# A fused RWKV-7 and HGRN2 layer on one core: bank order in the planner, the last column blocks of the output projection, and the layer norm

## The chip, the core and the metric

The kernel runs on one core of one Trainium2 chip. A core has five engines with instruction queues of their own: TensorE (PE, with weight loads shown as PEld) for matrix products, VectorE (DVE) and ScalarE (ACT) for elementwise work, GpSimd (POOL), and SyncE (SP), which here only issues DMA transfers. Each engine works through its queue in program order. Operands lie in SBUF; matrix products are summed up in PSUM, which has eight banks of 512 float32 columns on 128 partitions. The metric is device time in microseconds for one call, as the median of several runs. A profiled execution is a run of its own; its rows have times from the start of its span.

## What is computed

One layer with two groups of heads that read the same input `x` of 512 tokens by 2048 features: RWKV-7 time mixing and HGRN2 gated linear recurrence. Their gated outputs stand side by side and pass through one output projection, a residual and a layer norm:

```python
proj = einsum('btd,dc->btc', h, w_in)             # 2048 -> 8320 columns
o_rwkv = rwkv7(token_shift(proj[..., :RWKV_COLS])) * silu(z_r)
o_hgrn = hgrn2(proj[..., RWKV_COLS:]) * silu(z_h)
y = einsum('btc,cd->btd', concatenate([o_rwkv, o_hgrn], -1), w_out)
h = layer_norm(ALPHA * h + y, ln_w, ln_b)
```

The layer norm takes mean and variance of a token's 2048 values, then `(v - mean) * rstd * ln_w + ln_b`.

## The kernel before

**Products.** All large products are made with float32 values split in two float32r halves, hi and lo. `split` (L361) writes hi on ScalarE (`act` with a copy, in the trace L301) and lo = raw - hi on VectorE (`tt`, L311). `three` (L391, matmuls at L396) adds hi x hi, hi x lo and lo x hi into one PSUM bank, so each product costs three matmuls of 128 x 128 weights against 512 or 256 columns.

**Weights.** `load(j)` (L376) brings one row of `w_all`, 512 KB, into one of two raw buffers (`wr`). Each holds two quarters of 512 columns. `ready(i)` asks for the split of quarter i into a `wh` and a `wl` buffer (three of each); when the second quarter of a load is split, the load after the next goes out from SP's queue into the same buffer. `part(i)` waits, in the planner's time, until quarter i is split.

**The planner.** A class `Plan` writes the program order of all engines while the kernel is built. It keeps a clock per engine and for each tile when it was last written (`ready`) and last used (`busy`). Small tasks are Python generators in queues (`splits`, `evacs`, `scans`, `heads`, `sums`, `norms` and others); after each main matmul `pump` takes from them what could start by now. `start` gives the earliest start of an operation, `best` picks among the engines that could do it (a copy can go to ScalarE or VectorE), `issue` writes it down. For a read, `start` looks only at when the tile was written. For a write it also looks at the last use, but a write by TensorE looks at it only where the bank was just taken anew. The waits that the program has on the chip are placed by the framework from the real order of accesses; the planner's times only choose order and engine.

**Order of the work.** Projections run one after another on TensorE, and between their matmuls stand the small products of the RWKV scans (`rwkv_scan`, L288 and L292 in the trace), and of the HGRN2 heads. In a scan step the bank `pd` holds two results side by side: VectorE folds one into the state (`bd`), and copies of the other go to `z`. The bank `px` is read by a subtraction (`rt`), a copy and two additions (`t`).

**Output projection.** Its 2048 columns are done in five blocks, of 512, 512, 512, 256 and 256 columns. In the first four, `rows` runs over 16 steps of the inner dimension (eight of two for the 256 block), and in each over the four groups of 128 tokens, so four banks are open and the four token groups end close together. While the fourth block runs, the weights of the fifth are split too, some into free `t` buffers (`early`, `IN_T`). The fifth goes token group by token group, outermost, with all its weights there.

**Evacuation and norm.** `row_out` adds the residual (`xr`, loaded by `residual` from SP's queue) to a finished bank on VectorE (`stt`, L320), then takes statistics (`bn_stats`, L1336) and multiplies by `ln_w` (`premultiply`, L333, VectorE or GpSimd). After the fifth block of a token group, `finish` aggregates the statistics (L1279), and takes rstd as a power on GpSimd (L343). Then the columns are finished in two ways. `early`: the first `POOL_COLS[t]` columns are scaled and shifted on ScalarE (L1294), multiplied and added on GpSimd (L336), and written by SP. `late`: the others get two `scalar_tensor_tensor` on VectorE (less mean times weight, then times rstd plus bias) and are written from ScalarE's queue (L1310).

Of the kernel before, what the change touches and what calls it, by code (L numbers as in the profile page):

```python
# [15 lines left out]
P = 128  # L16
# [36 lines left out]

SETS = {AF.Sigmoid: ("sigmoid",), AF.Tanh: ("exp", "sigmoid"), AF.Exp: ("exp",)}


class Plan:
# [11 lines left out]
    def __init__(self, room):  # L69
        self.clock = {"pe": 0.0, "dve": 0.0, "act": 0.0, "pool": 0.0, "dma": 0.0}  # L70
        self.table = None
        self.narrow = False
        self.queues = []
        self.ready, self.busy = {}, {}
        self.room = room
        self.slots = {tag: [(0, 0.0)] * n for tag, n in room.items()}
        self.count, self.used = 0, {}

    def start(self, e, op):

        t = 0.0
        for r in op.reads:
            t = max(t, self.seen(r, e))
        for w in op.writes:
            x, by = self.busy.get(w, (0.0, e))
            if e != "pe" or by is None:
                t = max(t, x if by == e else x + self.AFTER[by])
        return t

# [117 lines left out]
def mixer_kernel(ctx, tc, x_t, x_r, w_all, par, up, ln_wb, consts, hmask, out):  # L207
# [25 lines left out]
    def take(tag, shape=(P, T), dt=F32):  # L233

        if not plan.free(tag):
            raise RuntimeError(f"no room: {tag}")
        slot = min(plan.slots[tag])
        plan.slots[tag].remove(slot)
        if tag in PBUFS:
            t = ppool.tile(list(shape), dt, tag=tag, name=nm(tag), bufs=PBUFS[tag])  # L240
        else:
            t = st(tag, list(shape), dt)
        name = t.tensor.name
        plan.busy[name] = (slot[1], None)
        tags[name] = tag
        return t
# [132 lines left out]
    def ready(i, tags=("wh", "wl")):  # L379
# [58 lines left out]
    def rows(q, width, lh, ll, fin, order=range(KT), hook=None, tags=("main",), early=None):  # L438
# [3 lines left out]
        for j in range(KT // per):  # L442
# [3 lines left out]
            for t in range(4):  # L446
                if j == 0:
                    pss.append(main_ps(tags)[:, :width])
                if early:
                    for i in early[j][t - 1 : t]:  # L450
                        ready(q + i, ("t", "t") if i in IN_T else ("wh", "wl"))
                elif 0 < t < 3:
                    ready(q + j + t)
# [614 lines left out]
    def first(q, tag):  # L1068
# [10 lines left out]
        def bring(c0, c1):  # L1079
# [3 lines left out]
            def run():  # L1083
                if q not in parts:
                    parts[q] = tuple(st(t, [P, QT], F32R) for t in ((tag, tag) if tag else ("wh", "wl")))
                hi, lo = parts[q]
# [161 lines left out]
    sums, earlies, norms = plan.queue(), plan.queue(), plan.queue()  # L1248
    stats = cpool.tile([P, 4, 5, 6], F32, tag="stats", name="stats")
# [3 lines left out]
    POOL_COLS = (768, 640, 512, 512)  # L1253
    blocks = [(0, 512), (512, 512), (1024, 512), (1536, 256), (1792, 256)]
# [6 lines left out]
    def cuts(c0, c1):  # L1261

        return [(max(c0, d * T), min(c1, d * T + T)) for d in range(4) if max(c0, d * T) < min(c1, d * T + T)]

# [3 lines left out]
    def premultiply(t, c0, c1):  # L1268

        c0 = max(c0, POOL_COLS[t])  # L1270
        if c0 < c1:
            y, w = ys[t][c0 // T][:, c0 % T : (c1 - 1) % T + 1], lnw[0][:, 0, c0:c1]
            k = y_keys(t, c0, c1)
            yield keyed(Op([dve_tt_way(y, y, w), pool_tt_way(y, y, w)], [], []), k, k)

    def finish(t):
        mv, rs = take("mv", [P, 4]), take("rs", [P, 1])
        k_st, k_mv, k_v, k_n, k_r, k_m = ([f"{n}{t}"] for n in ("stat", "mean", "var", "neg", "rstd", "bias"))
        yield keyed(Op([("dve", 0.1, lambda: dve.bn_aggr(mv[:, 0:2], stats[:, t]))], [], []), k_st, k_mv + k_v)  # L1279
        yield keyed(ts(mv[:, 1:2], mv[:, 1:2], LN_EPS, None, ALU.add), k_v, k_v)  # L1280
        yield keyed(ts(mv[:, 2:3], mv[:, 0:1], -1.0, None, ALU.mult), k_mv, k_n)
        yield keyed(rsqrt(rs, mv[:, 1:2]), k_v, k_r)

        def columns(c0, c1):
            y = ys[t][c0 // T][:, c0 % T : (c1 - 1) % T + 1]
            return y, lnw[0][:, 0, c0:c1], lnw[0][:, 1, c0:c1], out[t * P : t * P + P, c0:c1], y_keys(t, c0, c1)

        def early():

            yield keyed(pool_tt(mv[:, 3:4], mv[:, 2:3], rs, ALU.mult), k_n + k_r, k_m)  # L1290
            for c0, c1 in cuts(0, POOL_COLS[t]):
                y, w, b, o, k = columns(c0, c1)
                n = c1 - c0
                yield keyed(Op([("act", 0.28 + n * 0.00083, lambda: sc_e.activation(  # L1294
                    y, y, AF.Identity, scale=rs, bias=mv[:, 3:4]))], [], []), k + k_r + k_m, k)
# [19 lines left out]
    last_cols = (blocks[4][0], D)  # L1315

    def row_out(t, b, ps, xr, last=True):
        c0, n = blocks[b]
        d, o = c0 // T, c0 % T
        if o == 0:  # L1320
            ys[t][d] = yt[4 * t + d]
        y = ys[t][d][:, o : o + n]
        k = y_keys(t, c0, c0 + n)

        def run():
            yield keyed(stt(y, xr[:, o : o + n], ALPHA, ps, ALU.mult, ALU.add),
                        [xr.tensor.name, ps.tensor.name], k + [y.tensor.name])
            drop(ps)
            if last:
                drop(xr)  # L1330
            plan.add(sums, rest())
            if b == 4:
                plan.add(sums, finish(t))

        def rest():
            yield keyed(Op([("dve", 0.07 + n * 0.00105, lambda: dve.bn_stats(stats[:, t, b], y))], [], []),  # L1336
                        k, [f"stat{t}"])
            if b < 4:
                yield from premultiply(t, c0, c0 + n)
# [3 lines left out]
    def residual(t, c0, n):  # L1343
        xr = take("g")
        nc.sync.dma_start(xr, x_r[t, :, c0 : c0 + n])
        plan.fetched(xr, 4 * n)
        return xr

    xrs = {}

    def fin(t, ps, b):
        c0, n = blocks[b]
        if b == 0 and t == 0:
# [3 lines left out]
        row_out(t, b, ps, xrs[t], n == T)  # L1357

    def ahead(j, b):

        if b == 0:
# [6 lines left out]
        c0, n = blocks[b]  # L1368
        t = j - (KT // 2 if n == T else 0) - 3
        if 0 <= t < 4:  # L1370
            plan.until(room(g=1))
            xrs[t] = residual(t, c0, T)


    IN_T = (3, 4, 8, 9, 10, 11, 12, 13)
    early = ((2, 3, 4), (5,), (6,), (7, 8), (9, 10), (11, 12), (13, 14), (15,))
    for b in range(4):
        w = blocks[b][1]
        rows(4 * unit(w // P), w, gh, gl, lambda t, ps, b=b: fin(t, ps, b), korder, lambda j, b=b: ahead(j, b),
             ("main", "acc", "mix") if b else ("main",), early if b == 3 else None)  # L1380


    last = 4 * unit(2)
# [10 lines left out]
def _layout(inputs):  # L1394
# [72 lines left out]
```

## Time and profile before

| | us |
|---|---|
| median of three runs (lowest to highest) | 1121.27 (1120.59 to 1122.06) |
| the profiled execution | 1123.09 |
| its span, first to last instruction | 1121.3 |
| granted clock of TensorE, mean | 0.991 |

The profiled execution is 1.8 us over its span and 1.8 us over the median. In the rows of the profile, a group has its line, engine, operation, `out<-in` by the program's names, shape, count, then busy time, mean of one in ns, and the idle time before it with what ended it. A timeline row has start, duration and the same names. The name `q` or `inv` in the last stage is an output tile, `g` the residual, `big` the layer norm's weight and bias.

### The profile page before, as it was taken

To read this page: it belongs to the slowest core of one execution; us is meant where nothing else is said; L and a number is where in the kernel's file an instruction comes from. 1 tells how busy PE (TensorE), PEld (TensorE's weight loads), DVE (VectorE), ACT (ScalarE), POOL (GpSimd) and SP (SyncE) were. 2 spreads that over 40 slices of the span, in tenths; PEclk is the share of its full clock that TensorE was granted. 3 is DMA by queue.
4 is the path that set the end of the run, shared out by engine and by line. 5 is a ranking of instruction groups with operands and counts; after the bars stand their busy time and mean duration, and the time that the engine had idled before them with its cause. 6 is when DMAs were issued, how large, how long until landed. Compare 5 with 4: busy or idle time off the path is not lost.

```text
span 1121.3 us, 19205 instructions
## 1 busy us (share of the span) xinstructions
PE 1091.5 (97%) x7402; PEld 901.8 (80%) x7402; DVE 766.5 (68%) x1739; ACT 456.3 (41%) x1042; POOL 88.6 (8%) x163
## 2 busy tenths in 40 slices
PE   8999999999999999999999999999999999999994
PEld 7878878788888878788887888888887778888893
DVE  6658967645579767857986774657976776624468
ACT  6532365433332465534245552433346444322221
POOL 0000000000010000101000010001000010000015
PEclk8999999999999999999999999999999999999997
DMA  7222211133323311223231122322231145433433
GB/s 274 85 80 93 95 59 58 57 99 94 90 75 103 96 58 59 67 79 117 76 104 58 58 76 87 99 92 77 94 102 46 52 141 194 136 122 110 144 126 138
DMA packets 36667, 108.50 MB, mean 97 GB/s; under 512 B 4320, under 2 KB 6496, under 8 KB 36448
## 3 DMA queue, kind: packets, MB, share of 16 engines
q1 hardware_dynamic: 34848, 104.33, 29.2%
q10 hardware_dynamic: 1728, 2.95, 0.7%
q8 instruction: 58, 0.95, 0.4%
q14 instruction: 33, 0.27, 0.1%
HBM read 99.92 MB, written 7.34 MB: 96 GB/s over the span
## 4 chain that ended last, share of the span: by engine, by line
PE 89%; DVE 6%; ACT 2%; issue 1%; DMA 1%; POOL 0%; SPq 0%; DVEq 0%; ACTq 0%
PE main L396 68%; PE mix L288 10%; PE mix L396 3%; PE acc L396 3%; PE acc L288 3%; PE mix L292 2%; DVE q L320 1%; DVE wl L311 1%; DVE t L311 1%; ACT z L301 1%; DVE bd L320 1%; ACT wh L301 1%; DMA t<-x_t 0%; DVE inv L320 0%; DMA t<-spill 0%
## 5 line engine op out<-in xcount | busy, mean ns | idle before, releaser
L396 PE MATMUL main<-xh,wh 128*128 128x512 f32 x896 | 358.0, 400 | 2.2 <-ACT xh L301 2.2
L396 PE MATMUL main<-xh,wl 128*128 128x512 f32 x896 | 356.6, 398 | 0.0
L396 PE MATMUL main<-xl,wh 128*128 128x512 f32 x896 | 356.0, 397 | 0.0
L301 ACT ACTIVATE wh<-wr 128x512 fp32r<-128x512 f32 (+1 forms) x313 | 195.5, 626 | 268.9 <-PE main L396 203.9
L311 DVE TENSOR_TENSOR wl<-wr,wh 128x512 fp32r<-128x512 f32 (+1 forms) x313 | 213.5, 683 | 130.2 <-ACT wh L301 126.9
L396 PEld LDWEIGHTS main<-xh,wh 128*128 128x128 f32 x896 | 169.1, 189 | 36.0 <-ACT xh L301 2.6
L396 PEld LDWEIGHTS main<-xl,wh 128*128 128x128 f32 x896 | 168.9, 188 | 33.8 <-DVE xl L311 0.8
L396 PEld LDWEIGHTS main<-xh,wl 128*128 128x128 f32 x896 | 168.9, 189 | 33.5
L396 PE MATMUL main<-wh,xh 128*128 128x512 f32 (+1 forms) x272 | 108.0, 397 | 1.9 <-DVE t L320 1.9
L396 PE MATMUL main<-wh,xl 128*128 128x512 f32 (+1 forms) x272 | 108.1, 397 | 0.0
L396 PE MATMUL main<-wl,xh 128*128 128x512 f32 (+1 forms) x272 | 107.4, 395 | 0.0
L301 ACT ACTIVATE z<-mix 64x64 f32<-64x64 f32 (+1 forms) x245 | 56.0, 229 | 92.1 <-DVE bd L320 71.4
L396 PEld LDWEIGHTS main<-wh,xh 128*128 128x128 f32 x272 | 51.3, 189 | 10.4 <-DVE t L320 2.3
L396 PEld LDWEIGHTS main<-wh,xl 128*128 128x128 f32 x272 | 51.3, 189 | 8.6
L396 PEld LDWEIGHTS main<-wl,xh 128*128 128x128 f32 x272 | 51.3, 189 | 8.2
L302 ACT ACTIVATE t<-main,om 128x512 f32<-128x512 f32 x33 | 22.6, 688 | 61.2 <-PE main L396 61.1
L320 DVE SCALAR_TENSOR_TENSOR bd<-mix,pc,bd 64x64 f32<-64x64 f32 x112 | 31.2, 283 | 22.4 <-PE mix L288 17.2
L343 POOL TENSOR_TENSOR rs<-rs,mhalf 128x8 f32<-128x8 f32 (+1 forms) x16 | 25.1, 1572 | 250.3 <-DVE rs L316 129.5
L311 DVE TENSOR_TENSOR inv<-inv 64x30 f32<-64x30 f32 (+14 forms) x120 | 38.6, 322 | 3.1
L311 DVE TENSOR_TENSOR inv<-inv,inv 64x30 f32<-64x30 f32 (+14 forms) x120 | 38.6, 322 | 2.9
L346 POOL MEMSET z<- 64x128 f32 x64 | 11.9, 199 | 355.7 <-PE acc L288 312.1
L311 DVE TENSOR_TENSOR t<-t,tot 128x256 f32<-128x256 f32 x96 | 38.4, 416 | 0.2
(207 smaller groups left out, 1489.1 us busy)
## 6 DMA issues: line engine op xcount, KB each, us to landing
wr<-w_all SPq DMA_DIRECT2D x158, 512.0 KB, 3.5
t<-x_t SPq DMA_DIRECT2D x16, 256.0 KB, 5.6
g<-x_r SPq DMA_DIRECT2D x16, 256.0 KB, 4.2
spill<-g SPq DMA_DIRECT2D x12, 256.0 KB, 4.3
t<-spill SPq DMA_DIRECT2D x12, 256.0 KB, 4.0
big<-ln_wb SPq DMA_DIRECT2D x1, 2048.0 KB, 9.1
out<-q ACTq DMA_DIRECT2D x7, 256.0 KB, 2.4
up<-up SPq DMA_DIRECT2D x8, 128.0 KB, 2.8
```

The source lines that it names most:

```text
L288: return Op([("pe", cost, lambda: pe.matmul(o, l, r, start=start, stop=stop, **kw))], [l, r], [o], narrow=narrow)
L292: return Op([("pe", 0.11, lambda: pe.transpose(o, i, ident))], [i], [o])
L301: return "act", cost, lambda: sc_e.activation(o, i, f, scale=scale)
L302: return "act", cost, lambda: sc_e.activation(o, i, f, scale=scale, bias=bias)
L311: return dve_op([a, b], o, lambda: dve.tensor_tensor(o, a, b, f), base=0.16 if o.shape[0] < P and size(o) == C and o.tensor.name in tags e ...
L320: return dve_op([a, b], o, lambda: dve.scalar_tensor_tensor(o, a, s, b, f1, f2), per=0.00113, base=0.085 if o.shape[0] == P else 0.25 if s ...
L343: lambda: pool.tensor_tensor(o, i, mhalf[:, : size(o)], ALU.pow))], [i], [o])
L346: return Op([("pool", 0.1, lambda: pool.memset(o, v))], [], [o])
L396: pe.matmul(ps, l, r, start=first and i == 0, stop=last and i == 2)
```

## The change

Three things are changed.

1. **Planner.** PSUM banks are noted in `plan.banks`. A read of a bank may start only when the last use of that bank by another operation has ended (`done`), not only when it was written, and a write by TensorE takes account of the last use by another engine.
2. **Last two column blocks.** The output projection has four blocks of 512 columns. The first two run as before through `rows`. The third runs with token groups innermost, and in between the weights of the fourth are split, by quarters in the order of `_last_quarters`: (2, n) is a quarter of the third block, (3, n) one of the fourth. Those of the fourth go into `t`, `ksq` and `ia` buffers (`home`) and, for the last three, into `wh` and `wl`. The fourth runs with token groups outermost: 48 matmuls of 512 columns each. Its residual is loaded at the fourth of sixteen steps.
3. **Layer norm.** The multiplications and additions on GpSimd are gone. For token groups 0 to 2, ScalarE scales and shifts each of four 512-column pieces, and VectorE multiplies by the weight and adds the bias. For the last group the first two pieces (`AHEAD`) are multiplied by the weight as soon as they are evacuated, and after the statistics get the two `scalar_tensor_tensor`; the other two go over ScalarE. The bias -mean * rstd is made on VectorE; the power for rstd stays on GpSimd. All outputs are written from SP's queue.

The array of weights is laid out to match, by quarters in that order.

```diff
+def _last_quarters():
+
+    o = [(2, 0)] + [(d, n + 3 - d) for n in range(13) for d in (2, 3)]
+    return o + [(2, 14), (2, 15), (3, 13), (3, 14), (3, 15)]
...
             t = max(t, self.seen(r, e))
+            if r in self.banks:
+                t = max(t, self.done(r, e))
         for w in op.writes:
-            x, by = self.busy.get(w, (0.0, e))
-            if e != "pe" or by is None:
-                t = max(t, x if by == e else x + self.AFTER[by])
+            t = max(t, self.done(w, e))
         return t
+
+    def done(self, name, e):
+
+        x, by = self.busy.get(name, (0.0, e))
+        return (0.0 if e == "pe" else x) if by == e else x + self.AFTER[by]
...
+            plan.banks.add(t.tensor.name)
...
-            parts[i] = tuple(st(t, [P, QT], F32R) for t in tags)
+            parts[i] = home() if home else tuple(st(t, [P, QT], F32R) for t in ("wh", "wl"))
 
             def run():
                 yield from split(*parts[i], raws[i // 2][:, i % 2 * QT : i % 2 * QT + QT])
+                whole_parts.add(i)
...
-        plan.until(lambda: by_now(lo))
+        plan.until(lambda: i in whole_parts and by_now(lo))
...
-    sums, earlies, norms = plan.queue(), plan.queue(), plan.queue()
-    stats = cpool.tile([P, 4, 5, 6], F32, tag="stats", name="stats")
+    sums, norms = plan.queue(), plan.queue()
+    stats = cpool.tile([P, 4, 4, 6], F32, tag="stats", name="stats")
     ys = [[None] * 4 for _ in range(4)]
     yt = []
     lnw = []
-    POOL_COLS = (768, 640, 512, 512)
-    blocks = [(0, 512), (512, 512), (1024, 512), (1536, 256), (1792, 256)]
...
-    def premultiply(t, c0, c1):
-
-        c0 = max(c0, POOL_COLS[t])
-        if c0 < c1:
-            y, w = ys[t][c0 // T][:, c0 % T : (c1 - 1) % T + 1], lnw[0][:, 0, c0:c1]
-            k = y_keys(t, c0, c1)
-            yield keyed(Op([dve_tt_way(y, y, w), pool_tt_way(y, y, w)], [], []), k, k)
+    def premultiply(t, d):
+
+        if t == 3 and d < AHEAD:
+            k = y_keys(t, d * T, d * T + T)
+            yield keyed(tt(ys[t][d], ys[t][d], lnw[0][:, 0, d * T : d * T + T]), k, k)
+
+    AHEAD = 2
...
         yield keyed(rsqrt(rs, mv[:, 1:2]), k_v, k_r)
-
-        def columns(c0, c1):
-            y = ys[t][c0 // T][:, c0 % T : (c1 - 1) % T + 1]
-            return y, lnw[0][:, 0, c0:c1], lnw[0][:, 1, c0:c1], out[t * P : t * P + P, c0:c1], y_keys(t, c0, c1)
-
-        def early():
-
-            yield keyed(pool_tt(mv[:, 3:4], mv[:, 2:3], rs, ALU.mult), k_n + k_r, k_m)
-            for c0, c1 in cuts(0, POOL_COLS[t]):
-                y, w, b, o, k = columns(c0, c1)
-                n = c1 - c0
-                yield keyed(Op([("act", 0.28 + n * 0.00083, lambda: sc_e.activation(
-                    y, y, AF.Identity, scale=rs, bias=mv[:, 3:4]))], [], []), k + k_r + k_m, k)
-                yield keyed(pool_tt(y, y, w, ALU.mult), k, k)
-                yield keyed(pool_tt(y, y, b, ALU.add), k, k)
-                nc.sync.dma_start(o, y)
-
-        def late():
-            cols = [columns(*c) for c in cuts(POOL_COLS[t], D)]
-            yield from premultiply(t, *last_cols)
-            for i in range(len(cols) + 1):
-                if i < len(cols):
-                    y, w, b, o, k = cols[i]
-                    yield keyed(stt(y, w, mv[:, 2:3], y, ALU.mult, ALU.add), k + k_n, k)
-                if i:
-                    y, w, b, o, k = cols[i - 1]
-                    yield keyed(stt(y, y, rs, b, ALU.mult, ALU.add), k + k_r, k)
-                    nc.scalar.dma_start(o, y)
-
-        plan.add(earlies, early())
-        plan.add(norms, late())
+        first = [d for d in range(4) if t == 3 and d < AHEAD]
+        rest = [d for d in range(4) if d not in first]
+        if first:
+            yield small(ts(mv[:, 2:3], mv[:, 0:1], -1.0, None, ALU.mult), k_mv, k_n)
+
+        def less_mean(d):
+            y, w, b, o, k = columns(d)
+            return keyed(stt(y, w, mv[:, 2:3], y, ALU.mult, ALU.add), k + k_n, k)
+
+        def weighted(d):
+            y, w, b, o, k = columns(d)
+            return keyed(tt(y, y, w), k, k)
+
+        def last(d):
+            y, w, b, o, k = columns(d)
+            if d in first:
+                yield keyed(stt(y, y, rs, b, ALU.mult, ALU.add), k + k_r, k)
+            else:
+                yield keyed(tt(y, y, b, ALU.add), k, k)
+            nc.sync.dma_start(o, y)
+
+        def norm():
+            for d in first:
+                yield less_mean(d)
+            ahead = []
+            for d in first + rest:
+                if d in rest:
+                    yield lambda: f"scaled{t}_{d}" in done
+                    yield weighted(d)
+                ahead.append(d)
+                if len(ahead) > 1:
+                    yield from last(ahead.pop(0))
+            yield from last(ahead.pop(0))
+
+        plan.add(norms, norm())
+        yield small(stt(mv[:, 3:4], mv[:, 0:1], -1.0, rs, ALU.mult, ALU.mult), k_mv + k_r, k_m)
+        for d in rest:
+            y, w, b, o, k = columns(d)
+            yield keyed(Op([("act", 0.6, lambda y=y: sc_e.activation(
+                y, y, AF.Identity, scale=rs, bias=mv[:, 3:4]))], [], []), k + k_r + k_m, k)
+            done.add(f"scaled{t}_{d}")
...
+    banks = ("main", "acc", "mix")
+    for d in range(2):
+        rows(4 * unit(4), T, gh, gl, lambda t, ps, d=d: fin(t, ps, d), korder, lambda j, d=d: ahead(j, d),
+             banks if d else banks[:1])
+
+
+
+    q0 = 4 * unit(8)
+    seq = _last_quarters()
+    homes = {}
+
+    def home(n):
+        if n < 10:
+            return lambda: tuple(take("t", (P, QT), F32R) for _ in range(2))
+        if n == 10:
+            return lambda: tuple(take("ksq", (P, QT), F32R) for _ in range(2))
+        if n < 13:
+            def both():
+                if not homes:
+                    homes["ia"] = take("ia", (P, 4, QT), F32R)
+                return homes["ia"][:, 2 * (n - 11)], homes["ia"][:, 2 * (n - 11) + 1]
+
+            return both
+
+    def quarters(upto):
+        for i in range(min(upto, len(seq))):
+            d, n = seq[i]
+            ready(q0 + i, home(n) if d == 3 else None)
+
+    pss = []
+    for j in range(KT):
+        ahead(j, 2)
+        hi, lo = part(q0 + seq.index((2, j)), T)
+        for t in range(4):
+            if j == 0:
+                pss.append(main_ps(banks))
+            if 0 < t < 3:
+                quarters(seq.index((2, j + t)) + 1 if j + t < KT else seq.index((3, j + t - 3)) + 1)
+            sl = slice(t * P, t * P + P)
+            three(pss[t], gh[korder[j]][:, sl], gl[korder[j]][:, sl], hi, lo, j == 0, j == KT - 1)
+            if j == KT - 1:
+                fin(t, pss[t], 2)
     for t in range(4):
         sl = slice(t * P, t * P + P)
-        ps = main_ps(("main", "acc", "mix"))[:, :256]
+        ps = main_ps(banks)
         for n, k in enumerate(korder):
-            hi, lo = part(last + n // 2, 256)
-            three(ps, gh[k][:, sl], gl[k][:, sl], hi[:, n % 2], lo[:, n % 2], n == 0, n == KT - 1)
-        row_out(t, 4, ps, xrs[t])
+            if t == 0 and n == 1:
+                quarters(len(seq))
+            if n == 4:
+                residual(t, 3)
+            hi, lo = part(q0 + seq.index((3, n)), T)
+            three(ps, gh[k][:, sl], gl[k][:, sl], hi, lo, n == 0, n == KT - 1)
+        row_out(t, 3, ps)
     plan.until(lambda: not any(plan.queues))
...
-    for d in range(3):
+    for d in range(2):
         cols(wo, d * T, T, 2)
-    for d in (1536, 1792):
-        cols(wo, d, 256, 4)
+    last = [wo[n * P : n * P + P, d * T : d * T + T] for d, n in _last_quarters()]
+    units.append(np.stack([np.concatenate(last[i : i + 2], 1) for i in range(0, len(last), 2)]))
```

More of the change, by code (lines that the diff above doesn't have):

```diff
@@ L73, in __init__ @@
         self.queues = []
-        self.ready, self.busy = {}, {}
+        self.ready, self.busy, self.banks = {}, {}, set()
         self.room = room
@@ L436, in proj, with rows @@
         return ps
-    def rows(q, width, lh, ll, fin, order=range(KT), hook=None, tags=("main",), early=None):
+    def rows(q, width, lh, ll, fin, order=range(KT), hook=None, tags=("main",)):
         pss = []
@@ L448, in rows @@
                     pss.append(main_ps(tags)[:, :width])
[L449 to L452, printed above, removed]
+                if 0 < t < 3:
                     ready(q + j + t)
@@ L1312, in finish, with columns @@
-        plan.add(earlies, early())
-        plan.add(norms, late())
[L1315 to L1323, printed above, removed]
-        def run():
[L1326 to L1330, printed above, removed]
+        def columns(d):
+            c0, c1 = d * T, d * T + T
+            return (ys[t][d], lnw[0][:, 0, c0:c1], lnw[0][:, 1, c0:c1], out[t * P : t * P + P, c0:c1],
+                    y_keys(t, c0, c1))
@@ new lines, in small @@
+        def small(op, reads, writes):
+            op.ways = [("dve", 0.07, op.ways[0][2])]
+            return keyed(op, reads, writes)
+        yield keyed(Op([("dve", 0.29, lambda: dve.bn_aggr(mv[:, 0:2], stats[:, t]))], [], []), k_st, k_mv + k_v)
+        yield small(ts(mv[:, 1:2], mv[:, 1:2], LN_EPS, None, ALU.add), k_v, k_v)
+        yield keyed(rsqrt(rs, mv[:, 1:2]), k_v, k_r)
+        first = [d for d in range(4) if t == 3 and d < AHEAD]
+        rest = [d for d in range(4) if d not in first]
@@ L1341, in row_out, with residual, fin @@
         plan.add(evacs, run())
[L1343 to L1347, printed above, removed]
-    xrs = {}
-    def fin(t, ps, b):
-        c0, n = blocks[b]
-        if b == 0 and t == 0:
+    xrs = {}
+    def residual(t, d):
+        plan.until(room(g=1))
+        xrs[t] = take("g")
+        nc.sync.dma_start(xrs[t], x_r[t, :, d * T : d * T + T])
+        plan.fetched(xrs[t], 4 * T)
+    def fin(t, ps, d):
+        if d == 0 and t == 0:
@@ L1367, in ahead @@
                 plan.fetched(lnw[0], 8 * D)
[L1368 to L1380, printed above, removed]
```

36 lines of the change are left out of this document (21 added, 15 removed).

## The prediction

> **What bounds the kernel now.** I read the page first, then the busy time by stage, then the chain of work that ended last, then the last 65 us by engine.
>
> ```profile
> span 1121.3 us, 19205 instructions
> PE 1091.5 (97%) x7402; PEld 901.8 (80%) x7402; DVE 766.5 (68%) x1739; ACT 456.3 (41%) x1042; POOL 88.6 (8%) x163
> PE 89%; DVE 6%; ACT 2%; issue 1%; DMA 1%; POOL 0%; SPq 0%; DVEq 0%; ACTq 0%
> ```
>
> TensorE is busy 97% of the span and carries 89% of the chain, so time can be won in three places only: in the matmuls themselves, in TensorE's pauses, and after its last matmul. The table of stages (start:end, length, then busy time and instructions of PE, PEld, DVE, ACT, POOL, then clock, DMA share, GB/s) shows the pauses:
>
> ```profile
> 140.00:215.00 75.00, 73.16 (x858) 59.83 (x848) 53.97 (x180) 42.35 (x141) 3.04 (x13) 1.00 0.17 52
> 375.00:455.00 80.00, 77.96 (x841) 63.83 (x840) 55.94 (x172) 44.26 (x143) 2.98 (x13) 1.00 0.20 62
> 590.00:665.00 75.00, 73.77 (x741) 60.32 (x741) 54.45 (x180) 39.42 (x132) 6.38 (x13) 1.00 0.20 60
> 830.00:916.00 86.00, 83.64 (x807) 68.17 (x806) 59.38 (x180) 46.30 (x144) 4.60 (x13) 1.00 0.25 79
> 1081.50:1104.60 23.10, 23.03 (x192) 22.82 (x191) 21.07 (x43) 2.73 (x4) 12.05 (x13) 1.00 0.24 89
> 1104.60:1121.30 16.70, 0.00 (x0) 0.00 (x0) 12.87 (x17) 1.63 (x2) 7.74 (x8) 0.59 0.36 130
> ```
>
> The four stretches with the RWKV scans lose 1.84, 2.04, 1.23 and 2.36 us (length less PE), 7.5 us together. The tail of 16.7 us without a matmul is the largest single piece. In the timeline, the last two matmul rows and VectorE's rows of the last token:
>
> ```profile
> 1104.25 0.28 PE L396 MATMUL main<-wh,xl 128*128 128x256 f32 x1
> 1106.47 3.41 DVE L320 SCALAR_TENSOR_TENSOR q<-q,rs,big 128x512 f32<-128x512 f32 x2
> 1109.81 0.41 DVE L320 SCALAR_TENSOR_TENSOR inv<-g,main 128x256 f32<-128x256 f32 x1
> 1113.49 1.75 DVE L320 SCALAR_TENSOR_TENSOR inv<-big,mv,inv 128x512 f32<-128x512 f32 x1
> 1116.83 0.74 DVE L320 SCALAR_TENSOR_TENSOR inv<-inv,rs,big 128x512 f32<-128x512 f32 x1
> ```
>
> TensorE ends at 1104.53 (1104.25 + 0.28), VectorE starts the last token only at 1109.81, 5.3 us late, because it is still at token 2, and ends at 1117.57. From there to the end of the span are 3.73 us, the landing of the last output among them. The lateness has a cause: the same 512-column operation takes very different times in this stage (x is the count, then busy us, mean ns):
>
> ```profile
> L320 DVE SCALAR_TENSOR_TENSOR q<-q,rs,big 128x512 f32<-128x512 f32 x7 | 10.1, 1472 | 0.0
> L336 POOL TENSOR_TENSOR q<-q,big 128x512 f32<-128x512 f32 x6 | 9.6, 1595 | 3.0 <-ACT q L1294 2.8
> ```
>
> It is 0.74 alone (row at 1116.83) and 1.47 on average where GpSimd multiplies at the same time.
>
> **The change part by part.**
>
> *One block of 512 in place of two of 256.* The chain gives both spacings.
>
> ```profile
> 1014.94 43.52 PE main L396 x192
> 1081.49 5.77 PE main L396 x48
> 1058.30 0.28 PE L396 MATMUL acc<-wh,xh 128*128 128x256 f32 x1
> ```
>
> 192 matmuls of 512 columns take 43.52 us, 0.2267 each; one of 256 takes 5.77 / 48 = 0.1202, and 384 of them 46.16. The last stage begins at 1058.30 and would end at 1058.30 + 191 x 0.2267 + 0.39 (what one 512 matmul shows from start to end) = 1102.0 in place of 1104.53: **-2.5 us**.
>
> *The norm on VectorE and ScalarE.* Tokens outermost, each token has 48 x 0.2267 = 10.9 us of TensorE to itself. VectorE's work for it, from these rows:
>
> ```profile
> 1056.46 0.69 DVE L320 SCALAR_TENSOR_TENSOR q<-g,main 128x512 f32<-128x512 f32 x1 [2.04 <-PE main L396]
> 1057.18 0.69 DVE L1336 BATCH_NORM_STATS2 stats<-q 128x6 f32<-128x512 f32 x1
> 1097.82 0.74 DVE L320 SCALAR_TENSOR_TENSOR q<-big,mv,q 128x512 f32<-128x512 f32 x1
> 1098.48 3.48 DVE L320 SCALAR_TENSOR_TENSOR q<-q,rs,big 128x512 f32<-128x512 f32 x2
> 1073.59 1.29 DVE L311 TENSOR_TENSOR t<-wr,t 128x512 fp32r<-128x512 f32 x2 [3.49 <-ACT t L301]
> L1279 DVE BATCH_NORM_AGGREGATE mv<-stats 128x2 f32<-128x30 f32 x4 | 1.2, 291 | 0.1
> L343 POOL TENSOR_TENSOR rs<-mv,mhalf 128x1 f32<-128x1 f32 x4 | 3.0, 759 | 31.1 <-DVE mv L316 31.1
> L1294 ACT ACTIVATE q<-q,mv,rs 128x512 f32<-128x512 f32 x3 | 2.4, 816 | 15.2 <-POOL mv L336 15.2
> ```
>
> A step that needs the one before costs 0.72, a free tensor_tensor 0.61 (two in 1.29), a scalar_tensor_tensor 0.66 (1097.82 to 1098.48). For tokens 0 to 2: 0.72 + 0.72 + 0.33 + 0.25 + 8 x 0.61 = 6.9 us of 10.9, and ScalarE 4 x 0.82 = 3.3: VectorE is idle again before the next token ends, so the 5.3 us of lateness go. For the last token, counted from the last matmul: evacuation 0.72, statistics 0.72, aggregate 0.33, two small ones 0.23 make 2.0. GpSimd still has the power for rstd (0.76, start 2.0, ready 2.8); the first less-mean hides it, then the small bias: 2.9. Then less-mean 0.66, last 0.66, weight 0.61, last 0.66, weight 0.61, last 0.61, last 0.69 = 4.5. ScalarE's two scalings (2.95 to 3.8, and to 4.5) end before VectorE reaches them at 4.2 and 5.5. Sum 7.4 in place of 13.04 (1117.57 - 1104.53): **-5.6 us**. If this cover failed (the bias ahead of the less-means, say), rstd's 0.8 would show. The outputs go from ScalarE's queue to SP's; the last one still pays 3.73. On SP they stand beside the residual loads, which the code issues 2.7 us into a token (4 of 16 steps), while the first output of the token before is ready at 3.8 at the earliest (2.95 + 0.82, its scaling); so no residual queues behind an output. If one did wait behind the outputs, it would land some 1 us late and cost the tail that.
>
> The Trainium skill (SBUF — State Buffer, Who interferes with whom) says that a VectorE operation with two inputs in SBUF and a GpSimd operation that reads SBUF exclude one another for the whole instruction. By that rule the first less-mean would wait for the power, and the sum would be 0.7 us longer. The row below started inside a power that ran from 1088.77 to 1089.49 and took 0.48, so I do not add it.
>
> ```profile
> L320 DVE SCALAR_TENSOR_TENSOR q<-big,mv,q 128x256 f32<-128x256 f32 x1 | 0.5, 477 | 0.0
> ```
>
> *Weights for the last block split during the third.* 29 quarters of weights are split in 43.5 us where 16 were: a load (two quarters) per 2.72 us through the same two raw buffers, so each buffer must come round in 5.44. The nearest stage is the one from 1058, with about that pace:
>
> ```profile
> wr<-w_all SPq DMA_DIRECT2D x1, 512.0 KB, 3.5
> wr<-w_all SPq DMA_DIRECT2D x1, 512.0 KB, 5.4
> 1072.93 1.15 ACT L301 ACTIVATE t<-wr 128x512 fp32r<-128x512 f32 x2 [3.63 <-DMA wr<-w_all]
> 1074.92 0.33 SPq L376 DMA_DIRECT2D wr<-w_all  x1
> ```
>
> Landing 3.5 (the load alone; 5.4 where another load and a residual go beside it), then 1.99 from ScalarE's first half to the next load (1072.93 to 1074.92): 5.5 at best, 0.06 us over the need per round, and 6.5 rounds. A quarter is asked for 1.36 us into the step two ahead and is whole 2.0 later, which leaves 2.0 us. The first rounds also meet the evacuations of the block before (8 x 0.61 on VectorE). I take **+0.3 us**; ends 0 and, with 4.2 us a landing, +3 (6.5 x 0.75 - 2.0).
>
> *The planner.* It now lets no read of a bank start before the other engine's read ended, and no write before a read. That alters which engine gets a copy and where matmuls stand, from the first scan on; no row shows the new order, so it is bounded from both sides by the scans' idle time. For it:
>
> ```profile
> ACT z L301 <- DVE bd L320: 71.4, 44, 3.1
> PE acc L288 <- DVE t L311: 2.4, 8, 0.4
> 174.82 0.29 DVE L320 SCALAR_TENSOR_TENSOR bd<-mix,pc,bd 64x64 f32<-64x64 f32 x1
> 175.20 0.45 ACT L301 ACTIVATE z<-mix 64x64 f32<-64x64 f32 x2 [1.24 <-DVE bd L320]
> ```
>
> ScalarE stands 71.4 us behind VectorE's bd (44 times, in total), and in `rwkv_scan` both read one bank (`pd`), with no value passing from one to the other: the program does wait by bank, and the old plan did not know it. All of the 7.5 us of pauses would be the most to gain; a loss could be as large as what an unlucky order adds, which I bound by two thirds of the same, +5. I take a third as a gain, **-2.5 us**, nearer to the rows that show plan and program apart than to none.
>
> The sum: -2.5 - 5.6 + 0.3 - 2.5 = -10.3. The profiled execution took 1123.1, of that 1121.3 span, 1.8 over the median of 1121.27; on the median it gives **1111 us**.
>
> **The rivals.**
>
> *The planner gives nothing or costs.* Idle time of ScalarE costs nothing by itself, TensorE waited for such a read by name for only 2.4 us, and any reorder makes new pauses. The Trainium skill (PSUM — Partial Sum Buffer, PSUM bank collisions raise a hardware error) says that only accesses to one bank in the same 32-partition quadrant collide, so copies of the two 64-partition halves could run at once, and a plan by bank would hold back more than the chip needs. The row at 175.20 speaks against that here: the first of these two copies reads partitions 0 to 63 and still started only after the bd of partitions 64 to 127 (174.82 + 0.29), so the program waits by whole bank whatever the chip would allow. Time: 1121.3 - 7.8 + (0 to 5) = 1113.5 to 1118.5.
>
> *The planner takes nearly all pauses:* 1121.3 - 7.8 - 7.5 = 1106.
>
> *The feed of weights becomes the bound,* in the third block. If most landings took the 5.4 us of the crowded row, a round would be 7.4, and 6.5 x (7.4 - 5.44) - 2.0 = 10.7 us of stalls in TensorE: 1121.3 - 8.1 + 10.7 = 1123.9 with no gain of the planner, **slower than before**. It decides from a round of 7.0 us (6.5 x 1.56 - 2.0 = 8.1). For it: the crowded row. Against it: that row had a residual and a second load beside it, and the third block has residuals in four steps of sixteen only.
>
> *The norm stays late:* the power left on GpSimd, or an order in which VectorE stands for ScalarE, so that only the matmuls' 2.5 us and half of the tail go: 1121.3 - 2.5 - 2.8 = 1116.
>
> **How the numbers follow.** Forecast (1107.5 to 1113.5) 0.50; planner neutral or costly 0.28; nearly all pauses gone 0.08; feed 0.09; norm late 0.05. 0.2% is 2.2 us, about what a measurement of this kernel can tell from no change: faster means under 1119.0. Of the planner's 0.28 I leave 0.04 beyond its bound (0.03 same, 0.01 slower), of the feed's 0.09 0.02 same and 0.07 slower: faster 0.50 + 0.24 + 0.08 + 0.05 = 0.87, same 0.05, slower 0.08. The range, 1105 to 1118, takes the planner's and the feed's ends in and leaves the feed's worst out.
>
> **What would show it.** After the change: 192 last matmuls 0.227 apart and TensorE's end 2.5 us earlier against its own start of the block; 512-column operations on VectorE near 0.7 in the last 40 us; evacuation of the last token within 0.1 us of the last matmul and the last VectorE operation 7.4 after it; no idle of TensorE before `wh` or `wl` in the third block; less than 7.5 us of pauses in the four scan stretches, and fewer waits of ScalarE's z for VectorE's bd. Pauses above 7.5, or a third block over 43.5 us, make the prediction wrong upward.

## The result and the profile after

| | before | after |
|---|---|---|
| median of four runs each, us (lowest to highest) | 1120.93 (1120.41 to 1122.06) | 1095.22 (1094.58 to 1095.77) |
| ratio, 95% interval | | 0.9769 (0.9752 to 0.9786) |
| the profiled execution, its span, us | 1123.09, 1121.3 | 1095.77, 1094.0 |

25.7 us were won where 10.3 were forecast, and 1095.2 lies outside the range of 1105 to 1118. The page of the changed kernel, first part and the chain of work that ended last:

```profile
span 1094.0 us, 18706 instructions
PE 1079.4 (99%) x7210; PEld 893.3 (82%) x7210; DVE 767.6 (70%) x1781; ACT 452.7 (41%) x997; POOL 65.8 (6%) x145
PE 98%; DVE 1%; DMA 0%; SPq 0%; ACT 0%; DVEq 0%; issue 0%
```

The chain is the row to look at: TensorE's share rose from 89% to 98%, VectorE's fell from 6% to 1%, ScalarE's from 2% to 0%. The table of stages of the changed kernel has no pause left in the four scan stretches, nor in the stretch after them:

```profile
140.00:215.00 75.00, 75.00 (x818) 63.73 (x818) 56.95 (x193) 41.75 (x130) 2.92 (x12) 1.00 0.21 61
375.00:455.00 80.00, 80.00 (x830) 67.74 (x829) 61.92 (x198) 43.92 (x131) 3.49 (x14) 1.00 0.23 69
590.00:665.00 75.00, 75.00 (x753) 63.74 (x752) 56.95 (x187) 36.87 (x110) 4.73 (x11) 1.00 0.22 64
830.00:916.00 86.00, 86.00 (x811) 72.81 (x810) 69.53 (x210) 48.00 (x138) 7.51 (x14) 1.00 0.30 92
916.00:957.00 41.00, 41.00 (x199) 34.31 (x198) 26.47 (x45) 14.57 (x26) 1.38 (x1) 1.00 0.52 182
```

Where the span's 27.3 us went is read from the start of the same matmul in both timelines: the first of the output projection's second block, and of its last stage (256 or 512 columns). Before, then after:

```profile
971.26 0.39 PE L396 MATMUL acc<-wh,xh 128*128 128x512 f32 x1
```

```profile
951.73 0.39 PE L411 MATMUL acc<-wh,xh 128*128 128x512 f32 x1
...
1039.03 0.61 PE L411 MATMUL acc<-t,xh 128*128 128x512 f32 x2
...
1082.66 0.40 PE L411 MATMUL mix<-wh,xl 128*128 128x512 f32 x1
```

| stage, us | before | after | won |
|---|---|---|---|
| start to the second output block | 971.26 | 951.73 | 19.5 |
| second and third block | 87.04 | 87.30 | -0.3 |
| last stage, to TensorE's end | 46.23 | 44.03 | 2.2 |
| TensorE's end to VectorE's last | 13.04 | 7.25 | 5.8 |
| from there to the end of the span | 3.74 | 3.66 | 0.1 |

Not all of the 19.5 is the change's. The two profiled executions were 2.2 us over their median before and 0.6 after, and part of that difference is seen at their start: the 145th matmul of `three` begins at 45.10 us before and at 44.08 after, and the granted clock of the first 20 us was 0.83 and 0.91. From that matmul to the second output block 926.2 us became 907.7, so 18.5 were won there, where the forecast had 2.5. The rest of the surprise is thus in that first row, before the last two blocks begin; e1 below shows that the planner alone brings it. The last token group in the changed kernel's timeline of VectorE:

```profile
1083.10 0.69 DVE L332 SCALAR_TENSOR_TENSOR inv<-g,mix 128x512 f32<-128x512 f32 x1 [2.36 <-PE mix L411]
1083.82 0.69 DVE L1354 BATCH_NORM_STATS2 stats<-inv 128x6 f32<-128x512 f32 x1
1084.55 0.26 DVE L1296 BATCH_NORM_AGGREGATE mv<-stats 128x2 f32<-128x24 f32 x1
1084.85 0.21 DVE L328 TENSOR_SCALAR mv<-mv 128x1 f32<-128x1 f32 x2
1085.10 0.75 DVE L332 SCALAR_TENSOR_TENSOR inv<-big,mv,inv 128x512 f32<-128x512 f32 x1
...
1088.42 1.89 DVE L323 TENSOR_TENSOR inv<-inv,big 128x512 f32<-128x512 f32 x3
```

VectorE had been idle for 2.36 us when the last bank was ready (1082.66 + 0.40 = 1083.06) and began 0.04 later; before it was 5.3 us late. It ends at 1090.31.

### The profile page after: what moved, and what is told of

It is laid out like the page before. It is cut to its first block, busy times and chain, and to the rows that moved or that the text cites. A ratio compares the mean times of both kernels' runs of the same rounds, so it can differ in the third digit from the quotient of the medians.

```text
span 1094.0 us, 18706 instructions
## 1 busy us (share of the span) xinstructions
PE 1079.4 (99%) x7210; PEld 893.3 (82%) x7210; DVE 767.6 (70%) x1781; ACT 452.7 (41%) x997; POOL 65.8 (6%) x145
## 4 chain that ended last, share of the span: by engine, by line
PE 98%; DVE 1%; DMA 0%; SPq 0%; ACT 0%; DVEq 0%; issue 0%
PE main L411 75%; PE mix L300 11%; PE mix L411 4%; PE acc L411 4%; PE mix L304 2%; PE acc L300 2%; DMA t<-x_t 0%; DVE inv L332 0%; DVE inv L323 0%; SPq L1092 0%; DVE stats L1354 0%; DVE xl L323 0%; ACT xh L313 0%; DVEq L1515 0%; SPq L1114 0%
## 5 line engine op out<-in xcount | busy, mean ns | idle before, releaser
L313 ACT ACTIVATE wh<-wr 128x512 fp32r<-128x512 f32 (+1 forms) x308 | 192.2, 625 | 235.4 <-PE main L411 186.2
L323 DVE TENSOR_TENSOR wl<-wr,wh 128x512 fp32r<-128x512 f32 (+1 forms) x308 | 209.9, 682 | 91.3 <-ACT wh L313 88.6
L411 PE MATMUL main<-wl,xh 128*128 128x512 f32 x256 | 103.5, 404 | 0.0
L411 PE MATMUL main<-wh,xh 128*128 128x512 f32 x256 | 103.4, 404 | 0.0
L411 PE MATMUL main<-wh,xl 128*128 128x512 f32 x256 | 102.9, 402 | 0.0
L313 ACT ACTIVATE z<-mix 64x64 f32<-64x64 f32 (+1 forms) x179 | 41.9, 235 | 62.2 <-PE mix L304 30.4
L411 PEld LDWEIGHTS main<-wl,xh 128*128 128x128 f32 x256 | 48.2, 188 | 8.8 <-DVE wl L323 0.6
L411 PEld LDWEIGHTS main<-wh,xh 128*128 128x128 f32 x256 | 48.2, 188 | 8.5
L365 DVE COPY z<-mix 64x64 f32<-64x64 f32 (+1 forms) x141 | 31.9, 226 | 13.3 <-PE mix L300 11.0
L332 DVE SCALAR_TENSOR_TENSOR t<-main,pr,t 128x511 f32<-128x511 f32 x33 | 24.6, 747 | 21.2 <-ACT t L314 20.8
```

What stands on the lines that cost most here:

```text
L313: return "act", cost, lambda: sc_e.activation(o, i, f, scale=scale)
L323: return dve_op([a, b], o, lambda: dve.tensor_tensor(o, a, b, f), base=0.16 if o.shape[0] < P and size(o) == C and o.tensor.name in tags e ...
L332: return dve_op([a, b], o, lambda: dve.scalar_tensor_tensor(o, a, s, b, f1, f2), per=0.00113, base=0.085 if o.shape[0] == P else 0.25 if s ...
L365: f = lambda: dve.tensor_copy(o, i)
L411: pe.matmul(ps, l, r, start=first and i == 0, stop=last and i == 2)
```

## The experiments

Two questions: whether the planner alone won the unforeseen 16 us and by what, and what made VectorE's lateness go. The theory for the first: the program really waits by bank, the old plan did not know it, and so put small products into TensorE's queue before their input, or the bank that they write, was there. The rivals: the new blocks are needed for it; any more careful plan would do; the old order was just unlucky. The part of the rule that concerns writes of TensorE needed no run: the kernel before with that part alone is the same program as without it, instruction for instruction, and with the reads alone the same as with both.

### The parts alone

e1 is the kernel before with the planner's rule:

```diff
         for r in op.reads:
             t = max(t, self.seen(r, e))
+            if r in self.banks:
+                t = max(t, self.done(r, e))
         for w in op.writes:
...
+            t = max(t, self.done(w, e))
```

> The kernel before with the planner's rule on banks alone; output projection and norm as before. Theory: the 19.5 us by which the changed kernel reaches its second output block earlier (951.7 in place of 971.3) come from the planner alone, so 1120.9 - 19.5 = about 1101.5 (1099 to 1104). Rival, my forecast's size: the planner is worth 2.5, about 1118, and the rest of the 19.5 needs the new last blocks.

Measured 1103.43 us, ratio 0.9842 (0.9825 to 0.9858): 17.9 us. The rival falls; the planner alone does it. From the 145th matmul to the second output block e1 takes 907.9 us, the changed kernel 907.7, before 926.2. From TensorE's end to VectorE's last operation it takes 13.03 us, as before (13.04): the planner wins nothing there.

e4 is the changed kernel with those lines taken back to the old ones.

> The changed kernel with the old planner: only the last blocks and the norm are new. Theory: 2.2 us of TensorE, 5.8 of VectorE behind it and 0.3 lost in the third block, so 1120.9 - 7.8 = about 1113 (1111.5 to 1114.5). Rival: without the planner's knowledge the third block starves for weights or the tail is ordered worse, 1116 or more.

Measured 1111.98, ratio 0.9917 (0.9903 to 0.9932): 9.4 us, 1.6 more than the traces' 7.8 had said. The two parts add up to 27.3 against 25.7 for both. e4's own trace, from the 145th matmul on, is 8.6 us shorter than before's: the third block takes 43.5 us there, 43.8 in the changed kernel, and 0.6 are won ahead of the second output block. The other 0.8 are within the interval of e4's ratio, which reaches from 7.6 to 10.9 us.

### Which half of the rule

The rule acts twice: on which engine a copy is given to, and on the times that the planner goes on with. In e6 and e7, `best` works out both times, picks by one and returns the other (this is e6; e7 picks by the old times and returns those with the rule):

```diff
-            r = self.start(e, op)
...
+            for banks in (True, False):
+                r = self.start(e, op, banks)
...
+                both.append((s + cost, s, r, e, f))
+            c.append(both)
-        return min(c, key=lambda x: x[0])
+        return min(c, key=lambda x: x[0][0])[1]
```

> The kernel before; the rule on banks is used only to choose between ScalarE and VectorE, while the times the planner goes on with are the old ones. Theory A, the engine matters (a copy given to the engine that read the bank last waits for nobody): at least two thirds of the planner's gain, 1108 or less. Theory B, the times matter (products are put later in TensorE's queue, when their input is there): 1114 or more.

> The kernel before; the engine is chosen by the old times, but the planner goes on with the times that the rule on banks gives. Theory A (engine): at most a third of the gain, 1114 or more, or even slower, since the waits between the engines stay. Theory B (times): two thirds or more, 1108 or less.

e6 measured 1104.39 (ratio 0.985, 0.9835 to 0.9864), e7 1103.34 (0.9839, 0.9824 to 0.9853). Each half alone has nearly all of the 17.9. Neither theory predicted that: A fails in e7, B in e6. It suggests a floor: once TensorE hardly stalls, little is left for the other half to win. The chain agrees: from 45 to 890 us it is all TensorE in e1 and e7, and 97.9% TensorE in e6.

### Without the rule: one bank, more caution, moved constants

e5 leaves the planner as it was and ties only the copies from `pd` to z to VectorE, which reads that bank for bd anyway:

```diff
                 for h in range(2):
-                    yield copy(zs[(c + 1) % 3][0:64, hc[h]], block(pd, h, P))
+                    yield vcopy(zs[(c + 1) % 3][0:64, hc[h]], block(pd, h, P))
```

> The kernel before, old planner; only the copies from pd to z of the next scan chunk are tied to VectorE, the engine that reads that bank for bd. Theory: ScalarE's wait on bd in that one bank is what made the old plan wrong; ScalarE's z waiting for VectorE's bd falls from 71 us to under 25, and at least 10 of the 18 us go: 1111 or less. Rival: pd is one bank of several, or VectorE gets too much; 1117 or more.

Measured 1105.65, ratio 0.9866 (0.985 to 0.9881): 14.7 us, with the wait of ScalarE's z for bd gone from the list (its copies from that bank are VectorE's now). ScalarE's remaining z, from other banks, waits for products and no longer for bd.

e8 lets the planner know nothing of banks, but asks for more time ahead of TensorE's small products:

```diff
-    LEAD = -0.35
+    LEAD = -0.7
```

> The kernel before; the planner knows nothing of banks, but TensorE's small products are put in only when the plan has their inputs 0.7 us ahead in place of 0.35. Theory: it cannot know the extra wait, which is up to 3 us; ScalarE's z still stands over 40 us behind bd, and the gain is under 6: 1115.5 or more. Rival, any caution does: 1108 or less.

Measured 1104.82, ratio 0.9854 (0.9836 to 0.9873): 15.6 us. Here my theory failed and the rival held. In the waits of e8 (total us, times, longest), ScalarE still stands behind VectorE's bd:

```profile
ACT z L301 <- DVE bd L320: 38.3, 35, 2.3
```

So half of that wait can stay at almost no cost (e7 keeps 21.9 us of it). What costs, by the count of TensorE's stalls further down, is a product in TensorE's queue that is there too soon; knowing the wait avoids it, and so does a larger margin.

The controls move a constant that has nothing to do with banks: e9 and e12 what the planner adds after a ScalarE operation, e13 how early other engines' operations may start.

```diff
-    AFTER = {"pe": 0.2, "act": 0.145, ...
+    AFTER = {"pe": 0.2, "act": 0.16, ...      (e9; 0.13 in e12)
-    SLACK = 0.6
+    SLACK = 0.65                              (e13)
```

> A control: the kernel before with one constant of the planner moved a little (what it adds after a ScalarE operation, 0.145 to 0.16), which changes the order of some 2800 rows of TensorE's queue without any knowledge of banks. Theory: within 3 us of the kernel before, 1118 to 1124. Rival, the old order was just unlucky and any other is better: 1112 or less.

> A second control on the kernel before, without the rule on banks: what the planner adds after a ScalarE operation, 0.145 to 0.13, the other way than in the first control (which gained 5.8). Theory: without the rule the time depends on the order by chance and scatters from 1113 to 1123, always well above the 1103.4 with the rule. Rival: any order but the old one reaches about 1104.

> A third control on the kernel before: how early the planner lets an operation of another engine start, 0.6 to 0.65. Theory: 1113 to 1123, as the other controls. Rival: about 1104.

> The kernel before with the planner's rule on banks, and the constant of the first control (0.145 to 0.16). Theory: with the true waits known, TensorE hardly stalls in any order, so it stays within 2.5 us of the rule alone (1103.4): 1101 to 1106. Rival: the rule's 18 us are one lucky order, and a moved constant gives much of it back: 1108 or more.

e14 is e1 with the constant of e9.

| kernel | us | ratio (95%) |
|---|---|---|
| no rule, old constants | 1121 | 1 |
| no rule, e9 | 1114.56 | 0.9943 (0.9928 to 0.9958) |
| no rule, e12 | 1115.83 | 0.9955 (0.994 to 0.997) |
| no rule, e13 | 1125.68 | 1.0045 (1.003 to 1.006) |
| rule, e1 | 1103.43 | 0.9842 (0.9825 to 0.9858) |
| rule, e14 | 1102.71 | 0.9839 (0.9825 to 0.9854) |

e9 came out between its theory and its rival, and e13 2.7 above the 1123 I gave. Two of the three controls won 5.8 and 5.2 us, so the rival of an unlucky order holds for about a third of the 17.9. A blind plan scatters over 11 us with constants that have nothing to do with banks; a plan with the rule moved by 0.7, in the one constant tried. The waits and the chain tell the two kinds apart, e13 first, then e14:

```profile
ACT z L301 <- DVE bd L320: 57.3, 40, 2.7
PE 87%; DVE 6%; ACT 3%; issue 2%; DMA 1%; POOL 0%; SPq 0%; DVEq 0%; ACTq 0%
```

```profile
ACT z L307 <- DVE bd L326: 15.0, 13, 1.9
PE 96%; DVE 3%; DMA 0%; issue 0%; SPq 0%; DVEq 0%; ACT 0%
```

The time of before lies inside the scatter, so the rule is worth 17.9 us against this order, and 11 to 23 against the four blind ones. e5 and e8 are one order each; both lie some 9 us below the best of the blind four.

### What made VectorE late

e10 puts the multiplication by the norm's weight back on GpSimd in the changed kernel:

```diff
         def weighted(d):
             y, w, b, o, k = columns(d)
-            return keyed(tt(y, y, w), k, k)
+            return keyed(pool_tt(y, y, w, ALU.mult), k, k)
```

> The changed kernel with the multiplication by the norm's weight back on GpSimd (four 512-column pieces per token group, two for the last); all else as changed. Theory: VectorE's 512-column operations beside it take 1.0 us or more on average in place of 0.6 to 0.74, and the time from the last matmul to VectorE's last operation grows from 7.25 to 9 to 11: 1097.5 to 1099.5. Rival: the lateness before came from the short token interval of 5.8 us alone, not from GpSimd; the tail stays under 7.8 and the time at 1096 or less.

Measured 1095.35, the same as the changed kernel's 1095.22: the theory's 1097.5 to 1099.5 missed, and the time is the rival's. The groups of the last 45 us show VectorE's remaining additions in e10, and then both operations in the changed kernel:

```profile
L323 DVE TENSOR_TENSOR q<-q,big 128x512 f32<-128x512 f32 x12 | 17.3, 1501 | 6.8 <-POOL q L348 6.8
```

```profile
L323 DVE TENSOR_TENSOR q<-q,big 128x512 f32<-128x512 f32 x24 | 15.0, 686 | 2.7 <-ACT q L1337 2.7
```

Beside GpSimd an addition takes 1.50 us in place of 0.69, as expected; but there are half as many, so VectorE is busy 17.3 us with them in place of 15.0, and 10.9 us per token group hold that. The tail grew to 8.12, not to 9 to 11, and not under the rival's 7.8 either: VectorE has 0.23 us to spare when the last bank is ready, and only the last group's two pieces count in it. The 0.9 us that the tail grew do not show in the medians, whose runs spread over 1.2.

e11 puts the whole old norm (`premultiply`, `finish` with `early` and `late`) into the changed kernel, with its new blocks:

```diff
-    def premultiply(t, d):
+    def premultiply(t, c0, c1):
...
-        plan.add(norms, norm())
+        plan.add(earlies, early())
+        plan.add(norms, late())
...
+    last_cols = (1536, D)
+    POOL_COLS = (768, 640, 512, 512)
```

> The changed kernel (new planner, last block of 512 columns with token groups outermost) with the norm of before: GpSimd takes the first columns, VectorE the rest, outputs of the rest from ScalarE's queue. Theory after the run with the weight on GpSimd: the lateness went because a token group now has 10.9 us of TensorE in place of 5.8, not because GpSimd is gone; VectorE's tail falls from 13.0 to about 8 to 9.5, and the time is 1096 to 1098. Rival: the norm on GpSimd was what made VectorE late; the tail stays at 12 or more, 1100 or more.

Measured 1099.10 (1096.29 to 1100.40), ratio 0.9798 (0.9781 to 0.9814), 1.1 above what the theory gave; its profiled execution is the longest of the four. VectorE's rows of its last token group, and further down TensorE's weight loads waiting in the third block:

```profile
1086.40 0.69 DVE L332 SCALAR_TENSOR_TENSOR inv<-g,mix 128x512 f32<-128x512 f32 x1 [2.36 <-PE mix L411]
...
1092.54 2.41 DVE L332 SCALAR_TENSOR_TENSOR inv<-inv,rs,big 128x512 f32<-128x512 f32 x2
```

```profile
PEld main L411 <- DVE wl L323: 2.3, 5, 0.6
```

The lateness is gone with the old norm too, though VectorE is still slowed beside GpSimd (2.41 for these two, where two others in a row took 1.41): VectorE was idle 2.36 us before the last bank, and the tail is 8.58. The planner is no rival here, since e1, with the old blocks, keeps the tail of 13.03. So the 5.3 us of lateness went with the wider block and its 10.9 us per token group, where the 256 block gave half of that. Whether the new norm on the old blocks would have ended it as well was not run. The new norm itself is worth 1.3 us of the tail (8.58 - 7.25). What the theory had left out stands in the third block, 45.8 us here and 43.8 in the changed kernel: splits came late for TensorE's weight loads. Why the splits are later with the old norm was not followed up.

## Why the prediction was wrong

**The failed step** is the planner's bound: "All of the 7.5 us of pauses would be the most to gain". The gain was 17.9. The step read TensorE's pauses as the length less the busy time, in four stretches, and took a third of that. It had two faults. From the 145th matmul to the output projection, before takes 14.2 us longer than the changed kernel, and only 7.6 of these are idle time in its rows; the rest is inside what counts as busy. And the first output block, which still holds the small products of the last heads, was not among the stretches: it fell from 54.70 us (916.56 to 971.26) to 50.41 (901.32 to 951.73), 4.3, of which this row of before shows 2.3 as idle:

```profile
916.00:957.00 41.00, 38.71 (x240) 31.77 (x239) 29.69 (x67) 17.03 (x34) 5.56 (x3) 1.00 0.48 170
```

So of 18.5 us, 9.9 were idle time and 8.6 were hidden. A single stall in before's timeline of TensorE:

```profile
167.43 0.39 PE L396 MATMUL main<-wh,xl 128*128 128x512 f32 x1
168.12 0.49 PE L288 MATMUL acc<-bd,q 128*128 128x128 f32 x2 [0.31 <-DVE t L311]
```

Matmuls of 512 columns start 0.23 apart, and each row lasts 0.39. The next one started 0.69 after: 0.46 lost, of which the row shows 0.31 as idle and the busy time hides the rest. Counted by start to start from 45 to 900 us, each pair against the tenth percentile of pairs of its two shapes in before, before has 51 stalls over 0.16 us with 17.1 us in them; the changed kernel has 25 with 5.1, none over 0.21, all of one kind that before has too (24 with 4.9). That is 12 of the 14.2 us; the others are shorter. The same count goes with the times of the other runs: 21.6 us of stalls in e13, 13.0 in e12, 12.5 in e9, then 6.5 in e6, 6.4 in e5, 6.0 in e8, 5.1 in e1 and e7, and 4.9 in e14.

The chain of work had a bound on the page already that was not too low: 89% for TensorE leaves 11% of 1121 us, 123, and with the 16.7 of the tail away over 100 us. In the stretch from 140 to 215 us, the chain's shares by line, before and then after (the first is longer than shown):

```profile
by line: PE main L396 50.9%; PE mix L288 19.2%; PE acc L288 8.7%; PE mix L292 4.6%; ACT z L301 3.7%; DVE wl L311 2.5%; issue 2.4%; ACT wh L301 2.1%; DVE bd L320 1.9%; DVE t L311 1.6%; DVE nr L327 1.1%; DVE rt L320 0.5%; DVE t L353 0.4%; ACT
```

```profile
by line: PE main L411 67.1%; PE mix L300 20.8%; PE acc L300 8.9%; PE mix L304 3.5%
```

Before, TensorE's four entries make 83.4%, and 16.6% of 75 us, 12.4, run over other engines or issue where I had counted 1.84. That is an upper bound, since TensorE was busy for 73.16 of the 75 us; the truth lay between: the same 336 matmuls of `three` around this stretch (from 120.42 us before, 119.31 after) took 112.2 us before and 108.2 after. The share is no estimate: e5's chain has 91% TensorE, hardly more than before, and e5 is 14.7 us faster. I quoted the 89% and did not use it.

**The other steps**, in their order:

- One block of 512: forecast -2.5, measured -2.2 (46.23 to 44.03). Right.
- The norm and the lateness: forecast -5.6 with a tail of 7.4, measured -5.8 and 7.25. The size is right, and the token interval that the text named goes with the lateness (e11). But it also laid the lateness to GpSimd ("The lateness has a cause"); e10 and e11 show that the longer durations were real but, with the longer interval, not what decided. The bias stood between the two less-means as worked out. The first less-mean ran beside GpSimd's power and took 0.75 like those without it. By the rule that the Trainium skill gives (SBUF — State Buffer, Who interferes with whom), that the two exclude one another for a whole instruction, it would have waited for the power's end and finished 0.53 later (1085.63 less 1085.10, an estimate); the trace does not bear that out for this pair.
- Feed of the third block: forecast +0.3, measured +0.3. e11 shows that the margin is thin: 2.3 us more with another order.
- The planner by bank: the direction was right, and the row of 71.4 us pointed to a bank that matters (11.2 after, 10 times; e5 changes that bank alone). The size was off by a factor of seven. The rival that gave the planner nothing or a cost, and the one that took all pauses away at 1106, shared the wrong bound.
- SP's queue: no residual was late, as forecast.

Left open: whether a plan by bank and 32-partition quadrant would do as well was not tried, nor how much of the floor at 1103 another order could still win. Which wait of which bank made each single stall was not followed; the count shows only that the times go with the stalls.

## What to carry to other kernels

Estimate what better order can win by start-to-start times against the normal spacing, over every stretch that the order touches, and bound it by the share of the chain that runs over other engines; idle time is too low, since here the rows of 0.39 us at a spacing of 0.23 hid nearly half of the loss. A planner that writes an in-order queue must know the waits that the program will really have, or keep a margin for them; compare two plans only after moving a constant or two that should not matter. Before an engine is blamed for slow operations beside it, ask whether the stage has the time for them: with the longer interval per token group the lateness was gone, whether GpSimd multiplied or not.

## What the runs showed of the hardware

- Beside GpSimd's multiplications of 512 columns (four in 5.95 us in e10), VectorE's additions of two SBUF operands took 1.50 us in place of 0.69: in that stretch VectorE ended one per 1.44 us and GpSimd one per 1.49.
- GpSimd's power on 128x1 (1085.08 to 1085.63 in the changed kernel) left VectorE's less-mean, started at 1085.10, at 0.75 us, where the next two of its kind without it took 0.74.
- The planner's order and its choice between VectorE and ScalarE for copies moved this kernel by 11 us (1114.6 to 1125.7), with the same 7402 matmuls on TensorE and at most 37 copies more or fewer on ScalarE.
- The start of an execution went with the clock that TensorE was granted in its first 20 us. The changed kernel, e10 and e11 have the same order of matmuls there, and their 145th matmul of `three` began at 44.08 us (clock 0.91), 42.49 (1.00) and 45.22 (0.83).
